# Large tiles as 2 KB pieces of one pool, the differential gates behind the second q and k, merge projections with tokens stationary

## The chip, the cores and the metric

One NeuronCore of a Trainium2 chip runs the kernel. The metric is the device time of one execution in microseconds; before the change the median of three runs is 982.63 us (981.22 to 983.44). Engines: PE is TensorE (matmuls and transposes), ACT is ScalarE, DVE is VectorE, POOL is GpSimd, SP is SyncE, whose instruction stream issues all the DMAs.

## The reference

Two layers over 256 tokens of width 1024, batch 1, float32. Cut to what matters here:

```python
h = rmsnorm(x, norm_w)
proj = h @ w_in                       # 14368 columns, split among the branches below
# A) y_a = causal softmax attention with forget-gate bias (16 heads of 64) * silu(fg)
# B) y_b = Mamba-2 scan, gated by silu(sz), RMS-normed by group
# C) y_c = differential attention (8 heads, q and k each 2 x 64, v 128), partial rotary,
#          per-head RMSNorm, * silu(dg)
gates = sigmoid(mg).reshape(..., 3, 1024)
merged = sum(gates[n] * (branch[n] @ w_branch[n]) for n in range(3))
x = x + merged @ w_out                # after the second layer: out = rmsnorm(x, final_norm_w)
```

Everything is per token apart from the attentions, the convolution and the scan.

## The kernel before, in words

**Weights.** The weights of a layer are packed in the order of use as chunks of 1024 rows by 512 columns (two of them 272 columns). `load_chunk` (L211) brings a chunk in four units of 128 partitions x 1024 elements: a DMA into `raw` (4 buffers), then ACT copies it to `whi` in the rounded format fp32r (L227) and DVE subtracts to get the rest, `wlo` (L228). `whi` and `wlo` have 8 buffers each, so that two chunks can be in SBUF; a unit's buffer is free once its chunk's second pass has read it. An activation is split in the same way, and each product is three matmuls: hi x hi, hi x lo, lo x hi.

**Two forms of projection.** A chunk takes two passes, each into one PSUM bank of `pp` (3 buffers) of 128 x 512. In `bform` (L236) a pass holds 128 tokens: 128x128 pieces of the activation are the stationary operand and 512 weight columns stream, 24 matmuls a pass (L245), and tokens come out on the partitions. In `aform` (L249) a pass holds 256 weight columns: 128x128 pieces of the weights are stationary and 256 tokens stream, 48 matmuls a pass (L260), and channels come out on the partitions. Per layer 26 chunks use `aform`: q, k and gate of branch A, the inputs of the convolution, q and k of branch C, the six merge gates `mg` and the six merge projections `wb`; 11 use `bform`.

**Order.** `plan(l)` lists the chunks; the main loop goes through them, and after each pass `pump(BUDGET)` (L292) lets jobs add the work of the branches: attention heads (`fox_pair`, `diff_head`), the scan (`ssd_*`), the rotary step (`rope`) and transposes (`transposed`). A job is a generator; each step has a cost, and steps are taken until a pass has 3 units of it. This order gives priorities, from which a scheduler makes each engine's instruction stream, placing an instruction when its tiles have buffers. Each engine then takes its stream in order.

**The pool.** Nearly all large tiles are 128 partitions x 1024 float32 (4 KB a partition) from one pool `ap` with 20 buffers, named `a` in the trace: the split input `hT` (4), v, the gates, the head tiles of q (2 for four heads) and k (4), the split branch outputs `yA`, `yB`, `yC` (4 each), the merge gates `mg` (one a chunk), the merged sum. A tile waits until all readers of the tile that had its buffer are done.

**The merge.** `mg_evac` (L747) writes tanh of a merge gate's bank into its tile (ACT, L751). `wb_evac` (L801) multiplies the bank of a merge projection by its gate (DVE, L809), adds to the sum (L811), and after the third branch splits the sum (ACT L816, DVE L817) into `mT`, the stationary operand of the output projection `wo`. Sum and `mT` both have channels on the partitions.

**Branch C** has its chunks in this order: dq0, dk0, dv0, dv1, dg0, dg1, dq1, dk1, then mg1 (two chunks), wb1 (two), mg2, wb2, wo. dq0 and dk0 hold heads 0 to 3, dq1 and dk1 heads 4 to 7. `r_evac` copies the bank (L768), `rope` fetches the rotated rows by 16 small DMAs and 4 DVE instructions, and `split_qk` makes the head tiles (L372, L373 for q; L377 to L380 for k). A head scores (L396, L397), normalises, transposes (L685), multiplies by v (L692 to L694) and is normed and gated (L701).

Of the kernel before, what the change touches and what calls it, by code (L numbers as in the profile page):

```python
# [17 lines left out]
P = 128  # L18
# [31 lines left out]
def chunk_list():  # L50
# [8 lines left out]
             "sz0", "sz1", "dq0", "dk0", "dv0", "dv1", "dg0", "dg1", "dq1", "dk1",  # L59
# [37 lines left out]
def trunk(ctx: ExitStack, tc: tile.TileContext, x, norm_w, weights, small, vectors,  # L97
# [7 lines left out]
    ap = ctx.enter_context(tc.tile_pool(name="ap", bufs=20))  # L105
# [10 lines left out]
    def a4(shape=None):  # L116
        return ap.tile(shape or [P, 4, 256], F32, name="a4")

    def halves():
        return tuple([ap.tile([P, 4, 256], F32R, name="a4") for _ in range(2)] for _ in range(2))  # L120

    def at(half, kt):
        return half[kt // 4][:, kt % 4, :]
# [68 lines left out]
    def split_rows(src, hi, lo, tt, c):  # L192
        ps = bank(pt, "pt")
        for j in range(4):
            PE.transpose(ps[:, j * P:(j + 1) * P],
                         src[:, (4 * c + j) * P:(4 * c + j + 1) * P], ident)
        ts = slice(tt * P, (tt + 1) * P)
        return split_bank(ps.rearrange("p (j t) -> p j t", t=P), hi[c][:, :, ts], lo[c][:, :, ts])
# [5 lines left out]
    def norm_apply(xt, xs, r, wb, c):  # L204
        cs = slice(512 * c, 512 * c + 512)
        V.scalar_tensor_tensor(out=xs[:, cs], in0=xt[:, cs], scalar=r[:, 0:1], in1=wb[:, cs],
                               op0=ALU.mult, op1=ALU.mult)
# [59 lines left out]
    def make_h(l, tt, xt, xs, ss, gap):  # L267
        st = L[l]
        if tt == 0:
            st["hT"] = halves()  # L270
        with tc.high_priority(URGENT):
            r = norm_scale(ss)
            for c in range(2):
                norm_apply(xt, xs, r, st["nwb"], c)
        yield gap
        with tc.high_priority(URGENT):
            for c in range(2):
                st["split"] = split_rows(xs, st["hT"][0], st["hT"][1], tt, c)
        st[f"h{tt}"] = True

    def load_nwb(l):
        wb = a4([P, D])
        nc.sync.dma_start(wb, norm_w[l].partition_broadcast(P))
        L[l]["nwb"] = wb
# [90 lines left out]
    def stack_k(src, dst, dlo):  # L375
        for k, kl, main, rest in zip(dst, dlo, (LOH, HIH), (HIH, LOH)):
# [5 lines left out]
    def split_qk(key, src, tiles, jj):  # L382
        d = [t[:, 2 * jj:2 * jj + 2, :] for t in tiles]
        if key[1] == "q":
            stack_q(src, d)
        else:
            stack_k(src, d[0:2], d[2:4])

    def f4():
        return ap.tile([P, 4, 256], F32R, name="a4")  # L390

    def scores(st, pre, c, j, i, sc, bias, nm, rs):
        q, k, kl = st[f"{pre}q{c}"][i], st[f"{pre}k{c}"][i], st[f"{pre}k{c}"][2 + i]
# [18 lines left out]
    def fox_pair(l, b, yhi, ylo):  # L412
        st = L[l]
        c, j = b // 4, b % 4
# [10 lines left out]
        yield from need(l, f"fq{c}", f"fk{c}")  # L425
        nm = sm.tile([P, 2, 2], F32, name="nm")
        rs = sm.tile([P, 2, 2], F32, name="rs")
        for i in range(2):
            scores(st, "f", c, j, i, sc[:, i, :], sc[:, i, :], nm[:, i, :], rs[:, i, :])
# [8 lines left out]
        yield from need(l, "fv", f"fg{c}")  # L438
# [10 lines left out]
        for i in range(2):  # L449
            h = 2 * b + i  # L450
            r = slice(64 * i, 64 * i + 64)
            v0, v1 = st["fv"]
            PE.matmul(po[r, 0:T], lhsT=v0[:, h * 64:(h + 1) * 64], rhs=pTs[i][:, 0:T],  # L453
                      start=True, stop=False)
            PE.matmul(po[r, P:T], lhsT=v1[:, h * 64:(h + 1) * 64], rhs=pTs[i][:, T:384],  # L455
                      start=False, stop=True)
        yt = sc[:, 0, 0:T]
        V.tensor_tensor(out=yt, in0=po[:, 0:T], in1=st[f"fg{c}"][:, j, :], op=ALU.mult)
# [27 lines left out]
    def ssd_cb(l):  # L486
# [17 lines left out]
        for g in range(4):  # L504
            PE.transpose(ps[:, g * P:(g + 1) * P], bT[:, g, 0:P], ident)
# [7 lines left out]
    def ssd_x(l, c, tt):  # L513
# [21 lines left out]
    def ssd_group(l, g):  # L535
# [7 lines left out]
        if g == 0:  # L543
            st["xdd"] = a4([P, D])
            st["st0"] = a4([P, D])
        xdd, st0 = st["xdd"], st["st0"]
        xdt = [st["xdt0"], st["xdt1"]]
        y = [st["ys0"], st["ys1"]]
        ds = sm.tile([P, 4], F32, name="ds")
        V.tensor_tensor(out=ds, in0=dc[:, :, P - 1], in1=acs[:, 0, 4 * g:4 * g + 4], op=ALU.subtract)  # L550
        S.activation(out=ds, in_=ds, func=AF.Exp)
        gs = slice(256 * g, 256 * g + 256)
        for i in range(4):
            for b in range(2):
                bs = slice(b * P, (b + 1) * P)
                V.tensor_scalar(out=dc[:, i, bs], in0=dc[:, i, bs],
                                scalar1=acs[:, b, 4 * g + i:4 * g + i + 1], scalar2=0.0,
                                op0=ALU.subtract, op1=ALU.min)
        S.activation(out=dc, in_=dc, func=AF.Exp)
# [3 lines left out]
        V.tensor_tensor(out=dc, in0=dc,  # L563
                        in1=st["cb"][c][:, 2 * (g % 2):2 * (g % 2) + 2, :].rearrange("p b k -> p (b k)")
                        .unsqueeze(1).broadcast_to([P, 4, 256]), op=ALU.mult)
# [5 lines left out]
        for b in range(2):  # L571
            for i in range(4):
                h = 4 * g + i
                PE.matmul(ps[:, b * 256 + i * 64:b * 256 + (i + 1) * 64],  # L574
                          lhsT=dc[:, i, b * P:(b + 1) * P], rhs=xdt[b][:, h * 64:(h + 1) * 64],
# [5 lines left out]
        PE.matmul(ps[:, 0:256], lhsT=st["sC"][:, g, P:T], rhs=st0[:, gs], start=True, stop=True)  # L581
# [10 lines left out]
    def ssd_norm(l, tt):  # L592
        st = L[l]
        yield from need(l, "ysd", f"sz{tt}")
        y = st[f"ys{tt}"]
        V.tensor_tensor(out=y, in0=y, in1=st[f"sz{tt}"], op=ALU.mult)
        ss = sm.tile([P, 4], F32, name="ss4")
        for g in range(4):
            gs = slice(256 * g, 256 * g + 256)
            S.activation(out=st["xdt0"][:, gs], in_=y[:, gs], func=AF.Square, accum_out=ss[:, g:g + 1])  # L600
        r = rstd_of(ss, 256, 4.0 * EPS, 4)
        yield 1, 1.2
        for g in range(4):
            gs = slice(256 * g, 256 * g + 256)
            V.tensor_scalar(out=y[:, gs], in0=y[:, gs], scalar1=r[:, g:g + 1], scalar2=None, op0=ALU.mult)
# [4 lines left out]
    def transposed(l, name, y, scale):  # L610
        yield 1
        yhi, ylo = halves()
        for j2 in range(4):
            ps = bank(pt, "pt")
            for i in range(2):
                j = 2 * j2 + i
                for tt in range(2):
                    PE.transpose(ps[:, i * T + tt * P:i * T + (tt + 1) * P], y[tt][:, j * P:(j + 1) * P], ident)  # L618
# [10 lines left out]
    def rope(l, c):  # L629
# [4 lines left out]
        for hp_ in range(2):  # L634
            for t, src in enumerate((q, k)):
                for m in range(2):
                    b0 = 64 * hp_ + 32 * t + 16 * m
                    views.append((rp[b0:b0 + 16], src[64 * m:64 * m + 16, 2 * hp_:2 * hp_ + 2, :]))
# [11 lines left out]
        for key, src in ((f"dq{c}", q), (f"dk{c}", k)):  # L650
            tiles = [f4() for _ in range(2 if key[1] == "q" else 4)]
            for jj in range(2):
                split_qk(key, src[:, 2 * jj:2 * jj + 2, :], tiles, jj)
            st[key] = tiles
# [7 lines left out]
    def diff_head(l, h):  # L662
        st, pr = L[l], par[l]
        c, j = h // 4, h % 4
        yield from need(l, f"dq{c}", f"dk{c}")
# [3 lines left out]
        for i in range(2):  # L669
            scores(st, "d", c, j, i, sc[:, i, :], bmask, nm[:, i, :], rs[:, i, :])  # L670
# [10 lines left out]
        if "yd0" not in st:  # L681
            st["yd0"], st["yd1"] = a4([P, D]), a4([P, D])
# [17 lines left out]
        for tt in range(2):  # L700
            V.scalar_tensor_tensor(out=st[f"yd{tt}"][:, hs], in0=po[:, tt * P:(tt + 1) * P],  # L701
                                   scalar=r[:, tt:tt + 1], in1=st["dg"][tt][:, hs],
# [3 lines left out]
        if st["_d"] == 8 and "_dt" not in st:  # L706
            st["_dt"] = True
            start_job(transposed, l, "yC", [st["yd0"], st["yd1"]], lambda j: pr["subln"])

    def plan(l):  # L710
# [3 lines left out]
        def put(t, c0, ps, n):  # L714
            S.copy(out=t[:, c0:c0 + n], in_=ps[:, 0:n])

        def two(key):
            if key not in st:
                st[key] = [a4([P, D]) for _ in range(2)]
            return st[key]  # L720

        def v_evac(key, c0, n, last, extra=None):
            def f(tt, ps):
                put(two("_" + key)[tt], c0, ps, n)
# [11 lines left out]
        def gate_evac(key, c0, last):  # L736
            def f(tt, ps):
                t = two("_" + key)[tt][:, c0:c0 + 512]
                S.activation(out=t, in_=ps, func=AF.Tanh, scale=0.5)
                V.scalar_tensor_tensor(out=t, in0=t, scalar=1.0, in1=ps, op0=ALU.add, op1=ALU.mult)  # L740
                if last and tt == 1:
                    st[key] = st["_" + key]
                    for i in range(2):
                        st[f"{key}{i}"] = st[key][i]
            return f

        def mg_evac(nb, c):  # L747
            def f(jj, ps):
                if jj == 0:
                    st[f"mg{nb}{c}"] = a4()  # L750
                S.activation(out=st[f"mg{nb}{c}"][:, 2 * jj:2 * jj + 2, :],  # L751
                             in_=ps.rearrange("p (a t) -> p a t", t=T), func=AF.Tanh, scale=0.5)
            return f

        def t_evac(key):
            def f(jj, ps):
                if jj == 0:
                    st["_" + key] = [f4() for _ in range(2 if key[1] == "q" else 4)]
                split_qk(key, ps.rearrange("p (a t) -> p a t", t=T), st["_" + key], jj)
                if jj == 1:  # L760
                    st[key] = st["_" + key]
            return f

        def r_evac(key):
            def f(jj, ps):
                if jj == 0:
                    st["_" + key] = a4()
                S.copy(out=st["_" + key][:, 2 * jj:2 * jj + 2, :], in_=ps.rearrange("p (a t) -> p a t", t=T))  # L768
# [4 lines left out]
        def g_evac(key):  # L773
            def f(jj, ps):
                if jj == 0:
# [249 lines left out]
```

## Time and profile before

| | us |
|---|---|
| median of three runs (range) | 982.63 (981.22 to 983.44) |
| the profiled execution | 980.32 |
| its span, first to last instruction | 978.6 |
| PE busy / weight loads busy | 954.2 / 905.0 |
| DVE busy | 695.8 |
| ACT busy | 594.2 |
| DMA moved | 172.60 MB, mean 176 GB/s |

The profiled execution is 1.7 us longer than its span, and 2.3 us shorter than the median of the runs. A busy engine here is one with an instruction in it: matmuls overlap, and PE can be busy and yet not at its peak. The granted clock is PE's, as a share of 2.4 GHz.

### The profile page before, as it was taken

How to read it: one execution, taken by the hardware profiler on the slowest of the kernel's cores; microseconds unless marked ns; L12 is line 12 of the kernel's file. 1: busy time of each engine (PE TensorE's matmuls, PEld its weight loads, DVE VectorE, ACT ScalarE, POOL GpSimd, SP SyncE). 2: the span in 40 equal slices, each digit the busy share in tenths (PEclk: the TensorE clock that was granted, in tenths of full speed). 3: DMA queues.
4: the chain of work that ended last, by engine and by line, in shares of the span. 5: the costliest groups of instructions: out<-in, count | busy, mean ns of one | idle time of the engine just before them, and what ended most of it. 6: DMA issues, size and time to landing. Idle time of an engine off the chain costs nothing.

```text
span 978.6 us, 18423 instructions
## 1 busy us (share of the span) xinstructions
PE 954.2 (98%) x7044; PEld 905.0 (92%) x7044; DVE 695.8 (71%) x1398; ACT 594.2 (61%) x1117; POOL 36.2 (4%) x71
## 2 busy tenths in 40 slices
PE   8999999999999999989999999999999999999897
PEld 6999999999998999989889999999989889989895
DVE  6778788966667755785658768888856886557672
ACT  5677866643559644774546858765336785448542
POOL 1020000000000000000000110000000001000100
PEclk9999999999999999998999999999999999999899
DMA  7876454545555555453557655346555455463441
GB/s 241 287 248 183 138 166 161 184 173 173 176 180 183 175 182 183 158 172 122 186 183 241 210 180 172 113 162 222 176 183 185 154 188 182 144 233 130 130 152 43
DMA packets 57880, 172.60 MB, mean 176 GB/s; under 512 B 7040, under 2 KB 15552, under 8 KB 57792
## 3 DMA queue, kind: packets, MB, share of 16 engines
q1 hardware_dynamic: 57792, 171.43, 53.5%
q8 instruction: 55, 0.90, 0.4%
q14 instruction: 33, 0.27, 0.1%
HBM read 167.14 MB, written 2.16 MB: 173 GB/s over the span
## 4 chain that ended last, share of the span: by engine, by line
PE 95%; DMA 2%; DVE 1%; ACT 1%; issue 1%; POOL 0%; SPq 0%; POOLq 0%
PE pp L260 61%; PE pp L245 23%; PE pq L396 2%; PE pq L574 1%; PE pq L397 1%; PE pt L453 1%; PE pq L443 1%; PE pt L618 1%; DMA raw<-in_weights_dram 1%; ACT whi L227 1%; PE pq L685 1%; PE pt L455 1%; DMA scr<-sc_cum 0%; DMA sc<-scr 0%; PE pq L581 0%
## 5 line engine op out<-in xcount | busy, mean ns | idle before, releaser
L260 PE MATMUL pp<-a,whi 128*128 128x256 f32 x3328 | 620.1, 286 | 5.8 <-DVE a L809 4.6
L260 PEld LDWEIGHTS pp<-a,whi 128*128 128x128 f32 x3328 | 524.2, 193 | 9.3 <-ACT whi L227 3.4
L260 PE MATMUL pp<-a,wlo 128*128 128x256 f32 x1664 | 474.8, 286 | 0.0
L228 DVE TENSOR_TENSOR wlo<-raw,whi 128x1024 fp32r<-128x1024 f32 (+1 forms) x296 | 350.2, 1197 | 90.2 <-ACT whi L227 88.1
L227 ACT CAST whi<-raw 128x1024 fp32r<-128x1024 f32 (+1 forms) x296 | 300.8, 1026 | 149.4 <-PE pp L260 108.1
L260 PEld LDWEIGHTS pp<-a,wlo 128*128 128x128 f32 x1664 | 320.3, 193 | 0.4 <-issue 0.2
L245 PE MATMUL pp<-whi,a 128*128 128x512 f32 (+1 forms) x704 | 205.7, 374 | 1.2 <-ACT a L185 1.2
L245 PEld LDWEIGHTS pp<-whi,a 128*128 128x128 f32 x704 | 128.9, 189 | 24.1 <-ACT a L185 1.9
L245 PE MATMUL pp<-wlo,a 128*128 128x512 f32 (+1 forms) x352 | 130.0, 372 | 0.0
L245 PEld LDWEIGHTS pp<-wlo,a 128*128 128x128 f32 x352 | 66.2, 189 | 10.9 <-DVE wlo L228 0.3
L180 POOL TENSOR_TENSOR rstd<-rstd,mhalf 128x2 f32<-128x2 f32 (+2 forms) x26 | 19.3, 749 | 774.3 <-DVE rstd L178 774.3
L471 DVE SCALAR_TENSOR_TENSOR a<-sw,pT,a 128x255 f32<-128x255 f32 (+2 forms) x96 | 41.4, 479 | 3.3 <-ACT a L468 3.3
L396 PE MATMUL pq<-a,a 128*128 128x128 f32 (+1 forms) x128 | 31.8, 284 | 1.4 <-DVE nm L399 1.4
L402 ACT ACTIVATE sc<-sc,nm 128x128 f32<-128x128 f32 (+1 forms) x64 | 28.5, 447 | 5.3 <-DVE nm L399 5.1
L397 PE MATMUL pq<-a,a 128*128 128x128 f32 (+1 forms) x128 | 31.6, 269 | 0.0
L402 ACT ACTIVATE sc<-sc,dnm 128x128 f32<-128x128 f32 x64 | 28.5, 447 | 1.8 <-DVE dnm L399 1.8
L809 DVE SCALAR_TENSOR_TENSOR a<-a,pp 128x512 f32<-128x512 f32 x24 | 16.4, 684 | 18.5 <-PE pp L260 18.5
L768 ACT COPY a<-pp 128x512 f32<-128x512 f32 x16 | 9.3, 583 | 32.7 <-PE pp L260 32.7
L189 DVE SCALAR_TENSOR_TENSOR a<-pt,pT,a 128x256 fp32r<-128x256 f32 x32 | 14.5, 481 | 17.9 <-ACT a L188 17.7
L396 PEld LDWEIGHTS pq<-a,a 128*128 128x128 f32 x128 | 23.7, 191 | 2.2 <-DVE nm L399 1.6
L399 DVE CUSTOM_DVE_ANT_0 sc<-pq,sc 128x128 f32<-128x128 f32 (+1 forms) x64 | 19.5, 352 | 7.7 <-POOL sc L422 6.8
L397 PEld LDWEIGHTS pq<-a,a 128*128 128x128 f32 x128 | 23.6, 191 | 0.4
(163 smaller groups left out, 821.7 us busy)
## 6 DMA issues: line engine op xcount, KB each, us to landing
raw<-in_weights_dram SPq DMA_DIRECT2D x280, 512.0 KB, 4.4
raw<-in_weights_dram SPq DMA_DIRECT2D x16, 272.0 KB, 3.2
sc<-scr SPq DMA_DIRECT2D x16, 256.0 KB, 5.4
a<-scr SPq DMA_DIRECT2D x8, 512.0 KB, 6.1
sc<-scr SPq DMA_DIRECT2D x16, 128.0 KB, 4.9
a<-in_x_dram SPq DMA_DIRECT2D x4, 256.0 KB, 5.4
a<-in_norm_w_dram SPq DMA_DIRECT2D x2, 512.0 KB, 6.9
rp<-a SPq DMA_DIRECT2D x32, 32.0 KB, 3.0
```

The costliest lines, as they stand in the source:

```text
L180: G.tensor_tensor(out=r[:, 0:width], in0=r[:, 0:width], in1=mhalf[:, 0:width], op=ALU.pow)
L189: V.scalar_tensor_tensor(out=lo, in0=ps, scalar=scale, in1=hi.bitcast(F32), op0=ALU.mult, op1=ALU.subtract)
L227: S.copy(out=hi, in_=raw)
L228: V.tensor_tensor(out=lo, in0=raw, in1=hi.bitcast(F32), op=ALU.subtract)
L245: PE.matmul(ps[:, 0:n], lhsT=at(a, kt)[:, ts], rhs=w[:, k, 0:n], start=((u, k, i) == order[0]), stop=((u, k, i) == order[-1]))
L260: PE.matmul(ps[:, j * T:(j + 1) * T], lhsT=w[:, k, c0:c0 + P], rhs=at(a, kt), start=(kt == 0 and j == 0 and i == 0), stop=(kt == KT - 1 an ...
L396: PE.matmul(ps[:, o:o + n], lhsT=q[:, j, qs], rhs=k[:, j, 0:n], start=True, stop=False)
L397: PE.matmul(ps[:, o:o + n], lhsT=q[:, j, qs], rhs=kl[:, j, 0:n], start=False, stop=True)
L399: V.tensor_tensor_reduce(out=sc[:, sl], in0=ps[:, sl], in1=bias[:, sl], scale=-0.125, scalar=BIG, op0=ALU.add, op1=ALU.min, accum_out=nm[: ...
L402: S.activation(out=sc[:, sl], in_=sc[:, sl], func=AF.Exp, scale=-1.0, bias=nm[:, t:t + 1], accum_out=rs[:, t:t + 1])
L471: V.scalar_tensor_tensor(out=xc[:, s:T], in0=u[:, 0:T - s], scalar=pr["conv"](j, k), in1=xc[:, s:T], op0=ALU.mult, op1=ALU.add)
L809: V.scalar_tensor_tensor(out=t, in0=t, scalar=1.0, in1=p3, op0=ALU.add, op1=ALU.mult)
```

## The change

Five things. (1) The pool holds 41 tiles of 2 KB (128 x 512) in place of 20 of 4 KB; every large tile becomes two or four tiles, and instructions that covered 1024 columns become two. Head tiles of q and k now belong to two heads each, `fq0` to `fq3`, `dq0` to `dq3`. (2) dq1 and dk1 stand ahead of dg0 and dg1. (3) The six `mg` and six `wb` chunks of a layer go through `bform`; the gates and the sum have tokens on the partitions. (4) A new job `merge` transposes each token half of the sum by 8 PE transposes and splits it into `mT`; `wo` waits in the plan for the flag `mT0` or `mT1`. (5) The two chunks of wb2 form one item, so that both do their first pass before either does its second; the residual is loaded ahead of them instead of between them.

```diff
-    ap = ctx.enter_context(tc.tile_pool(name="ap", bufs=20))
+    ap = ctx.enter_context(tc.tile_pool(name="ap", bufs=41))
...
-    def a4(shape=None):
-        return ap.tile(shape or [P, 4, 256], F32, name="a4")
+    def a2(shape=None, dtype=F32):
+        return ap.tile(shape or [P, 2, 256], dtype, name="a2")
+
+    def rows():
+        return [a2([P, 512]) for _ in range(2)]
...
     def split_rows(src, hi, lo, tt, c):
         ps = bank(pt, "pt")
         for j in range(4):
+            PE.transpose(ps[:, j * P:(j + 1) * P], src[:, j * P:(j + 1) * P], ident)
         ts = slice(tt * P, (tt + 1) * P)
-        return split_bank(ps.rearrange("p (j t) -> p j t", t=P), hi[c][:, :, ts], lo[c][:, :, ts])
+        p4 = ps.rearrange("p (i j t) -> p i j t", i=2, t=P)
+        for i in range(2):
+            last = split_bank(p4[:, i], hi[2 * c + i][:, :, ts], lo[2 * c + i][:, :, ts])
+        return last
...
+    def spread(vec):
+        tiles = rows()
+        for c in range(2):
+            nc.sync.dma_start(tiles[c], vec[512 * c:512 * c + 512].partition_broadcast(P))
+        return tiles
...
-        dc = a4()
-        SMALL.dma_start(dc, st["scr"][16 + 4 * g:20 + 4 * g, :].partition_broadcast(P))
+        dc = [a2() for _ in range(2)]
+        for k in range(2):
+            r0 = 16 + 4 * g + 2 * k
+            SMALL.dma_start(dc[k], st["scr"][r0:r0 + 2, :].partition_broadcast(P))
...
         def mg_evac(nb, c):
+            def f(tt, ps):
+                if tt == 0:
+                    st[f"mg{nb}{c}"] = rows()
+                S.activation(out=st[f"mg{nb}{c}"][tt], in_=ps, func=AF.Tanh, scale=0.5)
+            return f
...
+        def merge(tt):
+            if tt == 0:
+                st["mT"] = halves()
+            yield 1
+            with tc.high_priority(URGENT):
+                for c in range(2):
+                    split_rows(st[f"m{c}"][tt], st["mT"][0], st["mT"][1], tt, c)
+            st[f"mT{tt}"] = True
+
         def wb_evac(nb, c):
+            def f(tt, ps):
+                t = st[f"mg{nb}{c}"][tt]
+                if nb == 0 and tt == 0:
+                    st[f"m{c}"] = st[f"mg{nb}{c}"]
+                m = st[f"m{c}"][tt]
+                V.scalar_tensor_tensor(out=t, in0=t, scalar=1.0, in1=ps, op0=ALU.add, op1=ALU.mult)
                 if nb > 0:
                     V.tensor_tensor(out=m, in0=m, in1=t, op=ALU.add)
-                if nb == 2:
-                    hi, lo = (z[c][:, js, :] for z in st["mT"])
-                    S.copy(out=hi, in_=m)
-                    V.tensor_tensor(out=lo, in0=m, in1=hi.bitcast(F32), op=ALU.subtract)
+                if nb == 2 and c == 1:
+                    start_job(merge, tt)
             return f
...
-                A(f"mg{nb}{c}", mg_evac(nb, c))
+                B(f"mg{nb}{c}", [mg_evac(nb, c)])
...
-                A(f"wb{nb}{c}", wb_evac(nb, c), act=lambda: st[key], wait=key)
+                B(f"wb{nb}{c}", [wb_evac(nb, c)], act=lambda: st[key], wait=key)
...
+        A("dq1", r_evac("dq1"))
+        A("dk1", r_evac("dk1"))
         for c in range(2):
             B(f"dg{c}", [gate_evac("dg", 512 * c, c == 1)])
-        A("dq1", r_evac("dq1"))
-        A("dk1", r_evac("dk1"))
...
-        for c in range(2):
-            A(f"wb2{c}", wb_evac(2, c), act=lambda: st["yC"], wait="yC", pre=load_res if c else None)
-        B("wo0", [wo_evac(0), wo_evac(1)], act=lambda: st["mT"])
+        B("wb20", [wb_evac(2, 0), wb_evac(2, 1)], act=lambda: st["yC"], pre=load_res, wait="yC")
+        B("wo0", [wo_evac(0), wo_evac(1)], act=lambda: st["mT"], flag="mT")
...
-                    if "h1" not in L[l] and s == 1:
-                        pump(0.0)
-                        assert "h1" in L[l]
+                    while f"{it['flag']}{s}" not in L[l]:
+                        pump(100.0)
```

## Rows read from the trace of the kernel before

**Rows 1.** The page: busy time, and the chain by engine and line.

```profile
PE 954.2 (98%) x7044; PEld 905.0 (92%) x7044; DVE 695.8 (71%) x1398; ACT 594.2 (61%) x1117; POOL 36.2 (4%) x71
...
PE 95%; DMA 2%; DVE 1%; ACT 1%; issue 1%; POOL 0%; SPq 0%; POOLq 0%
PE pp L260 61%; PE pp L245 23%; PE pq L396 2%; PE pq L574 1%; PE pq L397 1%; PE pt L453 1%; PE pq L443 1%; PE pt L618 1%; DMA raw<-in_weights_dram 1%; ACT whi L227 1%; PE pq L685 1%; PE pt L455 1%; DMA scr<-sc_cum 0%; DMA sc<-scr 0%; PE pq L581 0%
```

**Rows 2.** The chain in order of time: start us, length us, what, number of instructions.

```profile
187.12 11.52 PE pp L260 x96
...
468.96 21.80 PE pp L245 x96
...
756.68 0.87 PE pt L618 x8
```

**Rows 3.** Stretches: length; busy (instructions) of PE, PEld, DVE, ACT, POOL; clock; DMA.

```profile
187.12:198.63 11.51, 11.51 (x98) 11.51 (x98) 11.03 (x21) 7.09 (x11) 0.00 (x0) 1.00 0.54 164
...
386.40:407.00 20.60, 18.28 (x151) 18.11 (x151) 13.05 (x16) 10.86 (x14) 0.00 (x0) 1.00 0.43 142
...
435.00:449.30 14.30, 10.78 (x65) 9.89 (x64) 6.53 (x16) 6.31 (x19) 2.09 (x3) 0.76 0.35 112
...
442.00:444.00 2.00, 1.89 (x9) 1.89 (x10) 1.16 (x4) 1.22 (x3) 0.00 (x0) 0.50 0.00 0
...
915.90:930.20 14.30, 10.78 (x63) 9.89 (x62) 6.53 (x16) 6.12 (x19) 2.09 (x3) 0.76 0.35 111
...
345.10:449.30 104.20, 98.36 (x795) 97.10 (x794) 64.98 (x130) 59.56 (x120) 4.15 (x6) 0.97 0.51 165
```

**Rows 4.** What PE waited for: us in total, times, longest us.

```profile
PE pp L260 <- DVE a L809: 4.6, 4, 1.5
PE pt L692 <- DVE rstd L178: 4.4, 2, 2.2
```

**Rows 5.** ACT in order of time, gates and head tiles: start, length, instruction, count.

```profile
363.40 0.60 ACT L751 ACTIVATE a<-pp 128x512 f32<-128x512 f32 x1 [4.35 <-PE pp L260]
...
369.35 0.62 ACT L372 CAST a<-a 64x512 fp32r<-64x512 f32 x1 [2.13 <-DMA a<-rp]
...
398.33 1.09 ACT L751 ACTIVATE a<-pp 128x512 f32<-128x512 f32 x2 [0.84 <-DVE a L373]
...
403.52 0.62 ACT L377 CAST a<-a 64x512 fp32r<-64x512 f32 x1 [0.39 <-PE pp L260]
```

**Rows 6.** PE in order of time: first scores of heads 4 to 7.

```profile
407.04 0.22 PE L396 MATMUL pq<-a,a 128*128 128x128 f32 x1
```

**Rows 7.** DVE by instruction and shape: busy us, mean ns of one, idle before.

```profile
L228 DVE TENSOR_TENSOR wlo<-raw,whi 128x1024 fp32r<-128x1024 f32 x280 | 339.1, 1224 | 84.8 <-ACT whi L227 82.7
...
L809 DVE SCALAR_TENSOR_TENSOR a<-a,pp 128x512 f32<-128x512 f32 x24 | 16.4, 684 | 18.5 <-PE pp L260 18.5
...
L811 DVE TENSOR_TENSOR a<-a,a 128x512 f32<-128x512 f32 x16 | 11.0, 687 | 0.2
...
L701 DVE SCALAR_TENSOR_TENSOR a<-pt,rstd,a 128x128 f32<-128x128 f32 x32 | 9.7, 345 | 7.3 <-POOL rstd L180 7.2
...
L460 DVE TENSOR_TENSOR a<-sc,a 128x256 fp32r<-128x256 f32 x16 | 6.7, 421 | 1.3 <-ACT a L459 0.9
```

**Rows 8.** The chain at the start: start us, length us, what.

```profile
1.70 0.43 SPq L283
...
2.17 6.86 DMA raw<-in_weights_dram
```

**Rows 9.** What SP's queue waited for: us in total, times, longest us.

```profile
SPq L216 <- DVE a L560: 24.5, 2, 12.6
...
SPq L541 <- PE pp L260: 3.4, 3, 1.6
```

More of the change, by code (lines that the diff above doesn't have):

```diff
@@ L114, in trunk @@
     SMALL = nc.sync
-    def a4(shape=None):
-        return ap.tile(shape or [P, 4, 256], F32, name="a4")
+    def a2(shape=None, dtype=F32):
+        return ap.tile(shape or [P, 2, 256], dtype, name="a2")
+    def rows():
+        return [a2([P, 512]) for _ in range(2)]
     def halves():
-        return tuple([ap.tile([P, 4, 256], F32R, name="a4") for _ in range(2)] for _ in range(2))
+        return tuple([a2(dtype=F32R) for _ in range(4)] for _ in range(2))
     def at(half, kt):
-        return half[kt // 4][:, kt % 4, :]
+        return half[kt // 2][:, kt % 2, :]
     def bank(pool, name):
@@ L380, in stack_k, with split_qk, scores @@
             S.copy(out=kl[rest], in_=kl[main].bitcast(F32))
[L382 to L393, printed above, removed]
+    def split_qk(key, src):
+        tiles = [a2(dtype=F32R) for _ in range(2 if key[1] == "q" else 4)]
+        (stack_q if key[1] == "q" else stack_k)(src, tiles)
+        return tiles
+    def scores(st, pre, b, i, sc, bias, nm, rs):
+        j, tk = b % 2, st[f"{pre}k{b // 2}"]
+        q, k, kl = st[f"{pre}q{b // 2}"][i], tk[i], tk[2 + i]
         ps = bank(pq, "pq")
@@ L413, in fox_pair @@
         st = L[l]
-        c, j = b // 4, b % 4
+        hb, j = b // 2, b % 2
         yield from need(l, "scr")
@@ L424, in fox_pair @@
         yield 1, 0.0
-        yield from need(l, f"fq{c}", f"fk{c}")
+        yield from need(l, f"fq{hb}", f"fk{hb}")
         nm = sm.tile([P, 2, 2], F32, name="nm")
@@ L437, in fox_pair @@
         yield 2, 2.2
-        yield from need(l, "fv", f"fg{c}")
+        yield from need(l, "fv", f"fg{hb}")
         pTs = []
@@ L580, in ssd_group @@
         ps = bank(pq, "pq")
-        PE.matmul(ps[:, 0:256], lhsT=st["sC"][:, g, P:T], rhs=st0[:, gs], start=True, stop=True)
+        PE.matmul(ps[:, 0:256], lhsT=st["sC"][c][:, g % 2, P:T], rhs=st0[:, gs], start=True, stop=True)
         tmp = xdd[:, gs]
@@ L649, in rope @@
         yield 1, 2.4
-        for key, src in ((f"dq{c}", q), (f"dk{c}", k)):
-            tiles = [f4() for _ in range(2 if key[1] == "q" else 4)]
+        for key, src in (("dq", q), ("dk", k)):
             for jj in range(2):
-                split_qk(key, src[:, 2 * jj:2 * jj + 2, :], tiles, jj)
-            st[key] = tiles
+                st[f"{key}{2 * c + jj}"] = split_qk(key, src[jj])
             yield 1, 1.2 if key[1] == "k" else 2.4
@@ L712, in plan, with slot_of @@
         items = []
[L714 to L720, printed above, removed]
+        def slot_of(key, tt, c):
+            tiles = st.setdefault("_" + key, [{}, {}])[tt]
+            if c not in tiles:
+                tiles[c] = a2([P, 512])
+            return tiles[c]
         def v_evac(key, c0, n, last, extra=None):
             def f(tt, ps):
-                put(two("_" + key)[tt], c0, ps, n)
+                S.copy(out=slot_of(key, tt, c0 // 512)[:, c0 % 512:c0 % 512 + n], in_=ps[:, 0:n])
                 if extra:
@@ L756, in f @@
             def f(jj, ps):
[L757 to L761, printed above, removed]
+                st[f"{key[0:2]}{2 * int(key[2]) + jj}"] = split_qk(key, ps.rearrange("p (a t) -> p a t", t=T))
             return f
@@ L780, in f, with c_evac @@
                 V.scalar_tensor_tensor(out=t, in0=t, scalar=1.0, in1=p3, op0=ALU.add, op1=ALU.mult)
+                st[f"{key[0:2]}{2 * int(key[2]) + jj}"] = t
+            return f
+        def c_evac(key, j0):
+            def f(jj, ps):
+                t = a2()
+                u = tp.tile([P, 2, T], F32, name="sw")
+                S.copy(out=u, in_=ps.rearrange("p (a t) -> p a t", t=T))
+                for i in range(2):
+                    conv_tile(l, u[:, i, :], t[:, i, :], j0 + 2 * jj + i)
+                S.activation(out=u, in_=t, func=AF.Tanh)
+                V.scalar_tensor_tensor(out=t, in0=u, scalar=1.0, in1=t, op0=ALU.add, op1=ALU.mult)
+                st.setdefault("_" + key, []).append(t)
                 if jj == 1:
@@ L821, in f @@
             def f(tt, ps):
-                cs = slice(512 * c, 512 * c + 512)
                 xr = st["xres"][tt]
                 if c == 0:
-                    st[f"xs{tt}"] = (a4([P, D]), sm.tile([P, 4], F32, name="ss"))
+                    st[f"xs{tt}"] = (rows(), sm.tile([P, 4], F32, name="ss"))
                 xs, ss = st[f"xs{tt}"]
@@ L925, in trunk @@
     constants()
-    xt = [a4([P, D]) for _ in range(2)]
+    xt = [rows() for _ in range(2)]
     def load_x(tt):
```

201 lines of the change are left out of this document (84 added, 117 removed).

## The prediction

> **What bounds the kernel now.** I read the page first. PE has an instruction in it for 98% of the span, and 95% of the chain that ended last is PE: 61% from the matmuls of `aform` (L260), 23% from those of `bform` (L245) [rows 1]. DVE (695.8 us) and ACT have room on average. So the time is PE's stream: what its instructions cost, plus the places where it stands still. Both parts can be read.
>
> The first from the chain in order of time. An undisturbed `aform` chunk takes 11.52 us for 96 matmuls, 120.0 ns each for 256 columns; the two chunks of wo in `bform` take 21.80 us for 96, 227.1 ns each for 512 columns [rows 2]. Twice the columns cost 1.89 times as much: from the two, a column costs 0.418 ns and a matmul 12.9 ns beside its columns.
>
> The second from busy time by stretch. At 386.4 PE needs 20.60 us for 151 matmuls worth 18.1 at 120 ns: 2.5 lost. At 435.0 it needs 14.30 us for 65, worth at most 7.8: 6.5 lost, and there the granted clock is 0.76 on average and 0.50 from 442 to 444, the lower of PE's two levels (1.2 GHz), right after PE had waited [rows 3]. The second layer repeats it 480.9 us later (915.9: 14.30 us for 63) [rows 3]. That is 9.0 us a layer, 18.0 in all, between the k of branch C and the merge projection of branch C. I found nothing else of that size in the steady part.
>
> The waits name the cause of each: L260 on DVE's merge product L809, and L692 on a head's norm [rows 4]. ACT in order of time says why these come late. The gate of the first half of mg1 is written at 363.40, but both banks of the second half only at 398.33; the q head tiles of heads 4 to 7 start at 369.35 and the k ones at 403.52 [rows 5]. ACT was not full then. They had no buffer. By the program, at the second mg1 chunk the pool should hold hT 4, yB 4, v, the differential gates and the head outputs 2 each, the sum 2, the gates 2, raw k 1, q and k of four heads 6: 25 tiles in 20 buffers. So two PSUM banks of three are held by mg1 and PE waits for the third (the 2.5 us); and the scores of heads 4 to 7 come at 407.04 [rows 6], so that their tail and the transposes of yC meet the start of wb2 with no projection left to cover them (the 6.5 us).
>
> **The change part by part**, made against the profiled execution, 980.32 us (span 978.6, 1.7 around it).
>
> *Matmul form.* Per layer 12 chunks, 24 in all, go from 11.52 to 21.80/2 = 10.90 us: 24 x 0.62 = 14.9 us less. PE being the bound, all of it counts. Bounds: none of it if a gate in rows cost 240 ns for 512 columns, 14.9 if it costs what wo does; I take 14.9, since gates and wo would differ in their data only.
>
> The Trainium skill (TensorE: Matmul & The Clock Gate, Back-to-back issue gap) gives a lone matmul as N/2.4 plus about 2.5 ns, so 109.2 and 215.8 ns; by it a chunk falls from 10.48 to 10.36 us and 24 of them by 3 us only, a rule that speaks against this edit. The trace has 120.0 and 227.1 ns, and I go by these.
>
> *The transposes of the merge.* 8 for each of 2 token halves and 2 layers are 32; eight take 0.87 us [rows 2], so 32 x 0.109 = 3.5 us more on PE. The sum's split moves from L816/L817 to the PSUM side, 8 pieces of 256 columns a layer in place of 4 of 512: on DVE 8 x 0.42 against 4 x 0.69 [rows 7], 0.6 us a layer. The chain after the last wb2 pass (product 0.68, add 0.69, transposes 0.44 for a bank, ACT and DVE pieces of about 0.42) is some 3 us. In the plan it lies beside the first passes of wo, which need mT0 alone and last 10.9 us: cost nothing; without that cover 3 us a layer, and the lower clock behind it.
>
> *The pool and the order of dg.* Counted in the same way, the tiles live at any point of the new plan stay at or under 40 of 41, except around the second dg pass, 42 for a pass or two while the k of heads 4 to 7 is split. Counting the queue's cost of 3 a pass, the scores of heads 4 to 7 are added from the last dg pass to the second mg1 pass (before: from the last mg1 pass to the first of wb1), and yC's transposes in wb1 instead of mg2, five passes ahead of their use. So what made the 2.5 and the 6.5 goes: 18.0 us less. Bounds: 0 (all of it moves elsewhere) to 18.0.
>
> What is late next is DVE. From 345.1 to 449.3 it was busy 65.0 us [rows 3], some 30 of it units of weights at 1.22 (7 to 8 chunks), leaving 29. Of that about 21 (rotation, stacking, heads 4 to 7) now falls into nine passes of 5.45 us, with 18 units (22 us), the dg products (4 x 0.68) and the second half of heads 0 to 3 (4 x 0.9, from L701 and small pieces) [rows 7]: 49 us of DVE in 49 us. That is full. It need not stop PE: from 187.1 to 198.6 DVE was busy 11.03 of 11.51 us and PE did its 96 matmuls without a gap [rows 3], the banks allow a product to be late by two passes, and behind the stretch lie four mg2 passes with little to do. Bounds 0 to 9.0 a layer. I allow 2 us a layer, nearer the row without a gap: 4.0 us more.
>
> *Small pieces.* At the start the norm weights become two DMAs; one more issue of 0.43 us stands on SP ahead of the first weights, whose 6.86 us are on the path [rows 8]: 0.4 us more (0 to 0.5, or less than nothing if a half lands sooner). The scan's halved instructions (8 more of DVE and ACT each, at 0.1 to 0.2 us) lie beside PE: nothing. wb2 as a pair keeps both chunks' unit buffers through two passes, but wo and the first fv pair already do so behind each other: nothing. The residual's and the scan's DMAs, now 2 in place of 1, stand on SP ahead of weights; each needs a free tile, which the count above gives: nothing.
>
> **Sum:** 980.3 - 14.9 + 3.5 - 18.0 + 0.4 + 4.0 = 955.3 us for a profiled execution. The median of the runs shown stands 2.3 above the profiled one, so I predict 957.6.
>
> **The rivals.**
> *The stall moves.* The full DVE stretch makes products of dg or wb1 late, banks stay taken, and most of the 18.0 us turns up under dg and mg1, the lower clock with it. For: 49 in 49, and 42 tiles of 41. Against: the 11.03 of 11.51. Between 6 and all 18.0 us back, beyond the 4.0 allowed: 963 to 972 as a median.
> *The merge is not covered.* PE takes its stream in order; if merge's transposes stand ahead of wo's first pass, 3 us of wait plus 3.4 us of clock (0.24 of 14.3 us [rows 3]) come twice: 957.6 + 12.8 = 970.4. For: the transposes have high priority. Against: the same priority is used for hT at the layer boundary, where the chain shows wo undisturbed [rows 2].
> *Longer matmuls gain nothing in mg and wb*: if 512 columns cost 2 x 120 ns there, all 14.9 us are lost and the median is 972.5. The cadence of wo, which has the same operands' shapes, speaks against it [rows 2]. By the rule of the Trainium skill cited above (same page and section) 3 of the 14.9 us would stay.
> *Slower: SP stands.* The scan's second-half DMAs wait on SP for tiles while 38 to 40 of 41 are in use, in the passes of mg0, and the weights queue behind them. PE then has the chunk ahead, 10.9 us, in its unit buffers. The gain forecast is 25.0 us, 12.5 a layer; with 3.4 for the clock, a hold of 10.9 + 12.5 - 3.4 = 20 us a layer makes the kernel no faster, and one of 30 costs 22.5 a layer: 957.6 + 45 = 1003. Against: before, with 20 of 20 in use there, those loads held SP for 3.4 us in all, 1.6 at most, and the longest hold at weights behind the scan was 12.6 [rows 9].
>
> **How the numbers follow.** The forecast with 0 to 4 us lost a layer has 0.62, the moved stall 0.22, the merge 0.05, the gates 0.03, SP 0.05, and 0.03 that two of these add up to no change. The forecast's own range is 952 to 962. The whole range: down to 949 (no new stall, 953.6, and a part of the 3 us or so of smaller waits gone, a run at the low end), up to 972 where the old stall stays whole. That leaves some 0.15 outside. Faster by over 0.2% (what a measurement of this kernel can tell): 0.91; within it 0.03; slower 0.06.
>
> **What would show it.** Right: L260 falls to 2688 matmuls and L245 rises to 2208; mg and wb chunks take 10.9 us; the scores of heads 4 to 7 stand before wb1 on PE, L692 no longer waits there, and no stretch ahead of wb2 has a clock of 0.5; 32 more transposes at 0.11 us. Wrong: a wait of PE on L809, a gate's or a head's evacuation under dg or mg1 of more than 2 us a layer; a gap between wb2 and wo; ACT's weight copies waiting for DMAs while SP waits for a tile; or a row-form gate matmul at 240 ns.

## The result, and the profile after

The changed kernel takes 956.17 us (median of 4 runs, 955.31 to 958.41) against 983.04 (median of 4, 981.22 to 984.58) for the kernel before: ratio 0.9731, 95% interval 0.9707 to 0.9755. The forecast was 957.6 in 949 to 972. The profiled execution is 956.56 us with a span of 954.8 (before 980.32 and 978.6). By the medians the gain is 26.9 us. The profiled execution before lies 2.7 us under its median and the one after 0.4 over, so the two spans, on which all sums below are made, differ by 23.8 us only.

The page after, busy time, chain, and the groups of projection matmuls (L249 is `bform`, L264 `aform`):

```profile
PE 942.0 (99%) x5924; PEld 843.5 (88%) x5924; DVE 700.9 (73%) x1434; ACT 599.3 (63%) x1141; POOL 36.3 (4%) x71
...
PE 98%; DMA 1%; DVE 1%; ACT 0%; SPq 0%; POOLq 0%; issue 0%
...
L249 PE MATMUL pp<-whi,a 128*128 128x512 f32 (+1 forms) x1472 | 452.5, 387 | 1.9 <-ACT a L188 1.1
...
L264 PE MATMUL pp<-a,whi 128*128 128x256 f32 x1792 | 332.8, 284 | 0.0
...
L249 PE MATMUL pp<-wlo,a 128*128 128x512 f32 (+1 forms) x736 | 281.5, 385 | 0.0
L264 PE MATMUL pp<-a,wlo 128*128 128x256 f32 x896 | 255.2, 285 | 0.0
```

L264 has 1792 + 896 = 2688 matmuls and L249 1472 + 736 = 2208, and PE's share of the chain rose from 95% to 98% [rows 1]. The whole list of PE's waits after:

```profile
PE pq L930 <- POOL mhalf L147: 2.0, 1, 2.0
PE pt L198 <- DVE a L210: 2.0, 2, 1.5
PE pp L249 <- ACT a L188: 1.1, 1, 1.1
PE pp L249 <- ACT whi L231: 0.8, 1, 0.8
```

All four lie in the first 16 us. The waits on the merge product and on a head's norm [rows 4] are gone.

**Where the time went.** The chain gives the fixed points: the first fq0 matmul of each layer, a stretch of mg2 and wb2, the transposes of h, and the final norm. First after, then the kernel before (start, length, what):

```profile
40.97 19.30 PE pp L264 x161
...
421.93 25.90 PE pp L249 x114
...
478.78 0.87 PE pt L198 x8
...
506.94 19.30 PE pp L264 x161
...
947.96 0.77 DVE a L826 x2
```

```profile
36.82 18.35 PE pp L260 x153
...
516.09 19.32 PE pp L260 x161
...
971.86 0.77 DVE a L831 x2
```

Between them, the busy times of PE, PEld, DVE, ACT and POOL (instructions), the clock and the DMAs, by layer from fq0 to the next fixed point; before, then after:

```profile
36.82:516.09 479.27, 473.19 (x3513) 449.45 (x3512) 345.27 (x689) 294.65 (x550) 17.55 (x28) 0.99 0.55 178
516.09:971.86 455.77, 448.51 (x3350) 426.53 (x3349) 325.38 (x662) 275.90 (x521) 15.16 (x27) 0.99 0.52 169
```

```profile
40.97:506.94 465.97, 465.97 (x2953) 418.25 (x2952) 347.89 (x705) 296.74 (x562) 16.78 (x28) 1.00 0.57 183
506.94:947.96 441.02, 440.99 (x2791) 395.12 (x2789) 326.92 (x674) 278.23 (x529) 16.01 (x27) 1.00 0.54 175
```

Start +4.15, first layer 479.27 to 465.97 = -13.30, second layer 455.77 to 441.02 = -14.75, tail +0.1: -23.8 in all. In the layers PE stood idle for 6.08 and 7.26 us before; it stands idle for 0.00 and 0.03 after. It has 560 and 559 instructions fewer, as 576 fewer matmuls and 16 more transposes a layer should give.

Branch C after, PE in order of time: first scores of heads 4 to 7, the merge's transposes, the transposes of the next h.

```profile
367.08 0.31 PE L400 MATMUL pq<-a,a 128*128 128x128 f32 x1
...
447.67 0.60 PE L198 MATMUL pt<-ident,a 128*128 128x128 f32 x4
...
453.13 0.60 PE L198 MATMUL pt<-ident,a 128*128 128x128 f32 x4
...
461.56 0.60 PE L198 MATMUL pt<-ident,a 128*128 128x128 f32 x4
...
467.92 0.60 PE L198 MATMUL pt<-ident,a 128*128 128x128 f32 x4
...
478.62 1.04 PE L198 MATMUL pt<-ident,a 128*128 128x128 f32 x8
```

The scores come in the first mg1 chunk, 40 us earlier than in [rows 6]; the merge's transposes stand between matmuls with no gap ahead of or behind them.

### The profile page after: what moved, and what is told of

It reads as the page before. It is cut to its first block, busy times and chain, and to the rows that moved or that the text cites. A ratio compares the mean times of both kernels' runs of the same rounds, so it can differ in the third digit from the quotient of the medians.

```text
span 954.8 us, 16246 instructions
## 1 busy us (share of the span) xinstructions
PE 942.0 (99%) x5924; PEld 843.5 (88%) x5924; DVE 700.9 (73%) x1434; ACT 599.3 (63%) x1141; POOL 36.3 (4%) x71
## 4 chain that ended last, share of the span: by engine, by line
PE 98%; DMA 1%; DVE 1%; ACT 0%; SPq 0%; POOLq 0%; issue 0%
PE pp L249 51%; PE pp L264 34%; PE pq L400 2%; PE pt L457 2%; PE pq L583 1%; PE pq L401 1%; PE pq L447 1%; DMA raw<-in_weights_dram 1%; PE pt L627 1%; PE pt L198 1%; PE pt L458 1%; PE pq L692 1%; PE pq L590 0%; PE pt L700 0%; PE pq L499 0%; PE pt L699 0%
## 5 line engine op out<-in xcount | busy, mean ns | idle before, releaser
L249 PE MATMUL pp<-whi,a 128*128 128x512 f32 (+1 forms) x1472 | 452.5, 387 | 1.9 <-ACT a L188 1.1
L232 DVE TENSOR_TENSOR wlo<-raw,whi 128x1024 fp32r<-128x1024 f32 (+1 forms) x296 | 349.8, 1193 | 82.8 <-ACT whi L231 80.0
L264 PE MATMUL pp<-a,whi 128*128 128x256 f32 x1792 | 332.8, 284 | 0.0
L249 PEld LDWEIGHTS pp<-whi,a 128*128 128x128 f32 x1472 | 273.0, 189 | 55.3 <-ACT a L188 1.7
L264 PEld LDWEIGHTS pp<-a,whi 128*128 128x128 f32 x1792 | 281.5, 191 | 1.7 <-issue 1.4
L249 PE MATMUL pp<-wlo,a 128*128 128x512 f32 (+1 forms) x736 | 281.5, 385 | 0.0
L264 PE MATMUL pp<-a,wlo 128*128 128x256 f32 x896 | 255.2, 285 | 0.0
L264 PEld LDWEIGHTS pp<-a,wlo 128*128 128x128 f32 x896 | 171.5, 191 | 1.4 <-issue 1.4
L249 PEld LDWEIGHTS pp<-wlo,a 128*128 128x128 f32 x736 | 138.9, 189 | 25.8 <-DVE wlo L232 0.5
L188 ACT CAST a<-pt 128x256 fp32r<-128x256 f32 x32 | 11.5, 371 | 33.2 <-PE pt L198 27.0
L403 DVE CUSTOM_DVE_ANT_0 sc<-pq,sc 128x128 f32<-128x128 f32 (+1 forms) x64 | 19.5, 351 | 5.9 <-POOL sc L426 4.9
L191 ACT ACTIVATE a<-pt,pT 128x256 fp32r<-128x256 f32 x32 | 14.9, 473 | 14.1 <-PE pt L627 12.4
```

The source lines that it names most:

```text
L232: V.tensor_tensor(out=lo, in0=raw, in1=hi.bitcast(F32), op=ALU.subtract)
L249: PE.matmul(ps[:, 0:n], lhsT=at(a, kt)[:, ts], rhs=w[:, k, 0:n], start=((u, k, i) == order[0]), stop=((u, k, i) == order[-1]))
L264: PE.matmul(ps[:, j * T:(j + 1) * T], lhsT=w[:, k, c0:c0 + P], rhs=at(a, kt), start=(kt == 0 and j == 0 and i == 0), stop=(kt == KT - 1 an ...
L403: V.tensor_tensor_reduce(out=sc[:, sl], in0=ps[:, sl], in1=bias[:, sl], scale=-0.125, scalar=BIG, op0=ALU.add, op1=ALU.min, accum_out=nm[: ...
```

## The experiments

Theory, as the prediction had it: the stall of branch C is a lack of buffers, which the pool and the order of dg remove together; the matmul form is worth the columns' arithmetic; nothing is gained or lost at merge. Rivals: the form gains nothing; a stall of the same size has only moved; the order is the worse one, and the pool hides it.

**The form alone taken back.** mg and wb through `aform`, channels on the partitions, no merge job; pool and order of the change kept.

```diff
-                B(f"mg{nb}{c}", [mg_evac(nb, c)])
+                A(f"mg{nb}{c}", mg_evac(nb, c))
...
-                B(f"wb{nb}{c}", [wb_evac(nb, c)], act=lambda: st[key], wait=key)
+                A(f"wb{nb}{c}", wb_evac(nb, c), act=lambda: st[key], wait=key)
```

> The changed kernel with only the form of mg and wb undone: the 24 chunks go through aform again (48 matmuls of 256 columns a pass), gates and sum have channels on the partitions, the job merge and its 32 transposes are gone, wb2 is two items. Theory (the form is worth its cadence): 24 x 0.62 = 14.9 us come back, 3.5 us of transposes go, so 956.2 + 11.4 = 967.6 us, with no stall in branch C. Rival (the skill's N/2.4 + 2.5 ns a matmul, both forms nearly equal): 956.2 + 3.0 - 3.5 = 955.7. Rival (the form mattered by the buffers that it takes): stalls come back under mg1, over 972.

Measured 965.75 us, ratio 0.9845 (0.9825 to 0.9866): 9.6 us above the changed kernel by medians, 0.0114 x 983 = 11.2 by ratios. The fixed points in its trace (39.48, 510.80 and 957.27 us) say why the two differ: its layers take 471.32 and 446.47 us, 5.4 and 5.5 more than the change, 10.8 in all, but the start of that execution was 1.5 us shorter. The rival in which long matmuls gain nothing falls, and so does the one of the buffers (over 972).

The Trainium skill (TensorE: Matmul & The Clock Gate, Back-to-back issue gap) gives some 2.5 ns beside the columns for an isolated matmul, and says that in a stream the weight loads set the spacing too. Here every matmul has a weight load of its own, and 512 columns took 227.2 ns (25.90 us for 114 matmuls in mg2 and wb2), 11.4 more than the 215.8 of the isolated rule.

**The order of dg taken back**, all else as changed.

```diff
-        A("dq1", r_evac("dq1"))
-        A("dk1", r_evac("dk1"))
         for c in range(2):
             B(f"dg{c}", [gate_evac("dg", 512 * c, c == 1)])
+        A("dq1", r_evac("dq1"))
+        A("dk1", r_evac("dk1"))
```

> The changed kernel with dg0 and dg1 ahead of dq1 and dk1 again. Theory (pool and order together took the stall away): counted by the program 48 pieces are wanted at the second mg1 chunk where 41 are, so the k of heads 4 to 7 waits again, scores come late, and a part of the old 9.0 us a layer is back: 960 to 972 us, with a PE wait on wb1's product or on a head's norm. Rival (pieces alone were enough, since they come free earlier): 956 plus or minus 2, heads 4 to 7 scored in mg1. Rival (the order alone did it): the whole 18 us back, 972 to 975.

Measured 956.47 us, ratio 0.9742 (0.9728 to 0.9757), and no wait of PE in branch C. With 41 pieces the order is worth nothing that can be measured: the half of the theory that needed it falls, and the rival in which the pieces alone are enough is right.

**36 pieces in place of 41**, order and form as changed.

```diff
-    ap = ctx.enter_context(tc.tile_pool(name="ap", bufs=41))
+    ap = ctx.enter_context(tc.tile_pool(name="ap", bufs=36))
```

> The changed kernel with 36 pieces in the pool in place of 41 (72 KB, the old pool had 80). Theory (the count of live tiles sets when heads come and whether banks are held): 38 to 42 pieces are wanted in the scan and under dg, so tiles wait there; 960 to 975 us, with PE waits under mg0 or dg and a clock of 0.5 behind one. Rival (buffers no longer bind once heads have tiles by pairs): 956 plus or minus 2.

Measured 968.22 us, ratio 0.9864 (0.9849 to 0.9879), 12.05 us above the change. A stall is back in branch C: PE's waits in it, with the place they name,

```profile
PE pq L401 <- ACT a L388: 4.6, 4, 1.7
...
PE pq L400 <- DVE dnm L403: 1.9, 2, 0.9
```

are on the split k of branch C (L388) and on a DVE step of a head's scores (L403). So a lack of buffers is enough to stop PE here. It is not the old stall in its old place: in the first layer PE stands idle for 3.34 us between 360 and 380, under dg and the first mg1 pass, where it stood idle for 2.32 and 3.52 us from 386.4 and from 435.0 before [rows 3].

**wb2 as two items** in place of a pair.

```diff
-        B("wb20", [wb_evac(2, 0), wb_evac(2, 1)], act=lambda: st["yC"], pre=load_res, wait="yC")
+        for c in range(2):
+            B(f"wb2{c}", [wb_evac(2, c)], act=lambda: st["yC"], wait="yC", pre=load_res if c else None)
```

> The changed kernel with wb20 and wb21 as two items: each does both passes before the next, so the sum of the first token half is ready one pass (5.45 us) ahead of wo in place of two. Theory (the chain of merge is some 3 us and lies beside a pass in either case): 956 plus or minus 1.5, no gap between wb2 and wo. Rival (the pair is what covers merge): a wait of 3 us and a lower clock before wo in each layer, 962 to 969.

Measured 956.22 us, ratio 0.9741 (0.9726 to 0.9755): the pair is worth nothing, and the merge is covered either way.

**The start.** The 4.15 us there had no term of that size in the forecast. ACT after, in order of time: it copies the first half of a bank of h (L188), waits for DVE to have subtracted it (L189), and copies the second. Before that subtraction DVE still has a unit of weights to do (L232, 1.23 us from 11.38), so a turn is long.

```profile
10.31 1.04 ACT L231 CAST whi<-raw 128x1024 fp32r<-128x1024 f32 x1 [5.57 <-DMA raw<-in_weights_dram]
11.26 0.37 ACT L188 CAST a<-pt 128x256 fp32r<-128x256 f32 x1
12.98 0.65 ACT L188 CAST a<-pt 128x256 fp32r<-128x256 f32 x2 [1.35 <-DVE a L189]
14.17 0.37 ACT L188 CAST a<-pt 128x256 fp32r<-128x256 f32 x1 [0.54 <-DVE a L189]
```

So a bank split in two makes ACT and DVE take turns. Two edits: both copies ahead of both subtractions, and the first layer's norm weights by one DMA again.

```diff
-        for i in range(2):
-            last = split_bank(p4[:, i], hi[2 * c + i][:, :, ts], lo[2 * c + i][:, :, ts])
+        his = [S.copy(out=hi[2 * c + i][:, :, ts], in_=p4[:, i]) for i in range(2)]
+        for i in range(2):
+            v = V.tensor_tensor(out=lo[2 * c + i][:, :, ts], in0=p4[:, i], ...)
```

```diff
-        L[l]["nwb"] = spread(norm_w[l])
+        if l == 0:
+            wb = wsp.tile([P, KU * 512], F32, name="wlo")
+            nc.sync.dma_start(wb, norm_w[l].partition_broadcast(P))
+            L[l]["nwb"] = [wb[:, 0:512], wb[:, 512:1024]]
```

> The changed kernel with one edit in split_rows: both hi pieces of a bank are written first (ACT), then both lo pieces (DVE), in place of hi, lo, hi, lo. Theory (at the start ACT stands behind DVE twice, 1.35 and 0.54 us, so the second unit of weights is cast at 14.44 us and PE waits for it): 1.9 us earlier there, 954.3 us. Rival (the late landing of the first weights, 10.29 us against 9.03, is all of it): no change, 956.2 plus or minus 0.7.

> The changed kernel with layer 0's norm weights fetched by one DMA of 4 KB a partition again, into a free wlo buffer. Theory (the second DMA's issue and its slower transfer make the first weights land 1.3 us later): 1.3 us less, 954.9 us, first weights at about 9.0 us. Rival (what limits the start is ACT behind DVE in the split by halves): no change, 956.2 plus or minus 0.7.

Measured 954.75 us (0.9721, 0.9701 to 0.974) and 955.22 (0.9728, 0.9709 to 0.9746). The first has the direction expected, the second can't be told from the change: its first weights landed at 9.93 us, not at the 9.0 expected. Both edits together, beside these two, and then on the same chip the change itself and the first edit again:

> Both head edits of the two runs beside it. Theory (the 5.5 us by which the first pass ends later, 22.7 us against 17.2, come from these two things): 3.2 us by the sum of their waits, up to 5.5 if PE is fed in time behind them: 951 to 953 us. Rival (a third thing holds the start, such as the second half of x or the second unit's transfer): under 2 us in all.

> The changed kernel itself, timed again beside the three others of this call. Every theory: 956 plus or minus 1.5 us.

> The kernel with both hi pieces of a bank first, again, now beside the changed kernel on one chip. Theory (the 2.5 us by which its profiled span was shorter are real): 1 to 3 us under the changed kernel's median. Rival (what the start gains is given back by weights that land late): within 0.7 us of it.

Measured 955.22 us (both), 956.00 (955.34 to 956.81; the change again) and 954.25 (953.33 to 954.48; both copies first). The last two don't overlap: 1.75 us, and a version that is faster than both kernels, at 0.9717 (0.9696 to 0.9739) of the kernel before. ACT in it has no turns to wait for:

```profile
9.65 1.04 ACT L233 CAST whi<-raw 128x1024 fp32r<-128x1024 f32 x1 [5.42 <-DMA raw<-in_weights_dram]
10.61 1.19 ACT L201 CAST a<-pt 128x256 fp32r<-128x256 f32 x4
11.66 1.08 ACT L233 CAST whi<-raw 128x1024 fp32r<-128x1024 f32 x1
```

Its first layer is then 0.8 us longer (466.80 against 465.97), so the start itself gained more than that. Both together missed the 951 to 953 expected: fq0 begins at 37.19 us on PE there, 2.85 ahead of the repeated change (40.04), but PE in that kernel stops later, at the small sums of branch A,

```profile
55.05 0.28 PE L266 MATMUL pp<-a,wlo 128*128 128x256 f32 x1
57.17 0.59 PE L366 MATMUL pq<-sc_l,upper 128*128 128x16 f32 x4 [1.85 <-DVE sc_l L361]
```

and the first layer takes 468.57 us, 2.6 more than in the change, nearly all that the start had gained. Why DVE is late there wasn't pursued.

**Is the order good or bad where the pool is tight?** 38 pieces, with the new order and with the old one; and the pieces alone: 41, old order, `aform`.

> The changed kernel with 38 pieces. Theory (waits appear where the wanted count, up to 42, passes the pool; 36 pieces cost 12 us): between, 957 to 966 us, the wait again at the k of heads 4 to 7 beside dg. Rival (41 has room and only 36 goes under a threshold): 956 plus or minus 1.5.

> The old order of dg with 38 pieces. Theory (the order of dg is worth something only where the pool binds; with dg first 48 pieces are wanted under mg1): slower than 38 pieces with the new order by 3 us or more, since mg1's banks wait. Rival (the order is worth nothing at any size): within 1.5 us of 38 pieces in the new order. Rival (the new order is the worse one when the pool is tight, since k, q and dg then want pieces in the same passes): faster than it.

> The pool change alone: 41 pieces of 2 KB, with the old order of dg and with mg and wb in aform, as before the change. Theory (the pieces alone take the stall of branch C away, form and order apart): as the run with the channel form, 965 to 968 us, no PE wait on a merge product or a head's norm. Rival (form and pieces need each other, since aform's gates keep pieces longer): the stall is partly back, 970 to 980 us.

Measured 966.71 us (0.9847, 0.9823 to 0.987), 956.39 (0.9741, 0.972 to 0.9762) and 966.29 (0.9844, 0.9823 to 0.9865). With 38 pieces the new order has a stall, just over the 957 to 966 expected, and the old one none. Waits of PE with the new order:

```profile
PE pq L400 <- ACT a L387: 3.7, 2, 1.8
PE pp L249 <- ACT a L754: 2.6, 2, 1.3
```

The stretch from 360 to 380 us with the new order, then with the old:

```profile
360.00:380.00 20.00, 16.87 (x86) 14.10 (x86) 14.89 (x46) 15.71 (x45) 1.40 (x2) 0.91 0.59 183
```

```profile
360.00:380.00 20.00, 20.00 (x92) 16.62 (x92) 13.35 (x16) 12.28 (x18) 0.00 (x0) 1.00 0.60 209
```

and ACT with the new order, where the head tiles of k (L385, L387), the gate dg (L744) and mg1 (L754) are written within 3 us of each other, as they would be if they waited for the same pieces:

```profile
372.20 0.61 ACT L385 CAST a<-a 64x512 fp32r<-64x512 f32 x1
372.83 0.62 ACT L387 CAST a<-a 64x512 fp32r<-64x512 f32 x1
...
374.37 0.57 ACT L744 ACTIVATE a<-pp 128x512 f32<-128x512 f32 x1
374.85 0.58 ACT L754 ACTIVATE a<-pp 128x512 f32<-128x512 f32 x1
```

So the third rival is right: of the two orders the new one needs more pieces. That the pieces are what ties these four together is read from their times, not tested by itself. The pieces alone, in the chain (first fq0 of each layer, final norm):

```profile
40.72 19.30 PE pp L264 x161
...
512.28 19.30 PE pp L264 x161
...
958.87 0.77 DVE a L834 x2
```

471.56 and 446.59 us a layer: 7.7 and 9.2 less than before by the pieces alone, and 5.6 and 5.6 more than with the form as well.

## Why the prediction was right, step by step

**Form and transposes** (-14.9 + 3.5 = -11.4): measured -11.2, the two layers' 5.6 between pieces alone and the change (order and pair, which differ as well, being worth nothing), and -10.8 by the form alone. Right in mechanism and size.

**The stall** (-18.0): its place is shown by the waits that are gone, and its cause, tiles that find no buffer, from two sides. 41 pieces alone remove it; 38 in the old order (with the new form) do too, and they are 76 KB a partition where the old pool had 80, so it was not more memory that did it. And in the trace before, ACT starts on the last q head tiles of heads 4 to 7 (L372) when DVE has added a merge product (L811), with which they share no data; what that step can free is a tile:

```profile
396.35 1.14 ACT L372 CAST a<-a 64x512 fp32r<-64x512 f32 x2 [2.20 <-DVE a L811]
```

The second mg1 chunk is written right behind it, when the raw q has been read (L373, [rows 5]). A halved tile can also be read before its other half is written; no run separates this from buffers that come free sooner. Size: 13.30 + 14.75 - 11.2 = 16.9 us, the same as with the pieces alone (7.7 + 9.2). Of that, 6.08 + 7.26 - 0.03 = 13.3 is idle time of PE and the remaining 3.6 is not. The low clock of [rows 3], 3.4 us a layer by the prediction's own arithmetic, would more than account for it.

**"The pool and the order of dg"** as one step: this half was wrong. The order is worth nothing at 41 pieces and costs some 10 us at 38 (966.71 against 956.39). The count of live tiles that led to it was too high for the old order: by it 48 pieces were wanted, and with 38 there is no wait in branch C. Where the count went wrong wasn't measured.

**The allowance for DVE** (+4.0): nothing of it came. DVE in the stretch that I reckoned as "49 us in 49 us", the dq1 pass to the mg1 passes:

```profile
335.50:391.00 55.50, 55.50 (x289) 47.37 (x288) 42.80 (x97) 43.28 (x97) 2.79 (x4) 1.00 0.54 173
```

42.80 of 55.50 us, 77%, and PE full at clock 1.00. The rival of the moved stall falls with it.

**The start** (+0.4): the term that was mis-sized, by 3.75 us in the profiled execution. That execution is the slowest of nine whose kernels share this start: on PE the first fq0 matmul begins at 39.18 to 40.81 us in them (the change traced again: 40.04), against 36.66 in the one trace before, so the loss is 2.5 to 4.15 us. The DMA issue is there (first weights issued at 2.65 us against 2.17, [rows 8]), but the kernel without it begins fq0 at 39.52, within that range. What I had no term for is the split of a bank into pieces: "small pieces" lie beside PE elsewhere, and here nothing covers them yet. With both copies first fq0 begins at 37.38 and 37.82, ahead of all nine. PE from its first projection matmul to fq0, before, after, and with both copies first:

```profile
10.64:36.82 26.18, 25.94 (x154) 23.22 (x155) 19.68 (x36) 18.19 (x36) 0.56 (x1) 0.93 0.77 262
```

```profile
11.68:40.97 29.29, 28.47 (x154) 24.37 (x155) 20.81 (x41) 19.19 (x40) 0.56 (x1) 0.85 0.74 232
```

```profile
11.03:37.98 26.95, 26.93 (x154) 23.75 (x155) 20.82 (x42) 18.89 (x40) 0.56 (x1) 0.90 0.80 264
```

It is the same number of instructions in all three. After the change they begin 1.04 us later and take 3.11 us longer: 0.58 us of it is more idle time (0.82 against 0.24), and in the other 2.53 PE is busy at a lower mean clock, 0.85 against 0.93. So the turns are most of the loss; by the medians both copies first give 1.75 us back. How the rest divides between the DMA and the clock stays open.

**What is a loss only in part.** From fq0 to the scan the change takes 2.9 us longer in the first layer. The stretch before, then after:

```profile
36.82:158.89 122.07, 122.07 (x1005) 117.57 (x1004) 97.57 (x235) 88.25 (x178) 7.99 (x16) 1.00 0.59 190
```

```profile
40.97:165.93 124.96, 124.96 (x1016) 119.25 (x1015) 97.90 (x233) 89.50 (x181) 7.88 (x16) 1.00 0.58 186
```

PE is busy throughout in both, at a clock of 1.00, and has 11 instructions more in the second: seven projection matmuls and four transposes that stood behind the scan's first step now stand ahead of it. They are some 1.3 us (7 x 0.12 + 0.44). The other 1.6 us the same instructions take longer; this is a real loss, counted in the layer sums above, and its cause wasn't pursued. A fixed point must be one that no work passes; the fq0 matmuls are.

**Merge, SP:** PE waits for neither, as forecast. So the sum on the spans: -11.4 came as -11.2; -18.0 + 0.4 + 4.0 = -13.6 came as -16.9 + 4.15 + 0 = -12.75. The total is right partly by luck: the allowance not needed and the start not foreseen cancel. The last step, 2.3 us from a profiled execution to a median, did not hold either: the profiled execution came 1.3 us over its forecast (956.56 against 955.3) and the median 1.4 under (956.17 against 957.6).

## What to carry to other kernels

When PE waits for tiles in a full pool, count what is held in the units in which it is let go: here 76 KB in halves removed a stall that 80 KB in whole tiles had, and a reorder made for it was worth nothing, or harmful where the pool was tight. Ahead of cutting tiles, look for the place where no other work covers the pieces, such as the kernel's first instructions, and there let each engine do all its pieces before the next engine takes turns with it. After a change, measure between points that no work can pass, see that the instruction counts between them agree, and take a second trace where a short stretch decides: here the start differed by 1.6 us among nine.

## What was not expected of the hardware

A matmul of 512 columns took 227.2 ns in mg2 and wb2, as in wo before (227.1), so the 12.9 ns beside the columns that the prediction had worked out hold there too. At the start, the same 154 PE instructions kept PE busy for 25.94 us at a mean granted clock of 0.93 in one trace and for 28.47 us at 0.85 in another. Idle time alone does not tell which it will be: with 38 pieces and the new order PE idled longer there (1.63 us against 0.82), at a clock of 0.94. And with DVE busy for 97.90 of 124.96 us in branch A and ACT for 89.50, PE was never idle.
